# A two-layer decoder trunk on one core: opening on x by columns, and folding attention's two key blocks into one

## The chip, the cores and the metric

The kernel runs on one core of a Trainium2 chip. TensorE (PE in the profile; PEld is its weight load) multiplies, VectorE (DVE) and ScalarE (ACT) do the elementwise work, GpSimd (POOL) does a little of it, and SyncE's queue (SP) issues nearly all DMA. The metric is device microseconds of one execution. Three runs of the kernel before took 1168.31, 1168.37 and 1169.77 us, median 1168.37 us.

## What is computed

x is 256 tokens of 1024 features in float32. Two layers follow one another, each with an FFN of half weight, a mixing sub-layer and a second FFN:

```python
def rms_norm(x, g):
    y = x32 * lax.rsqrt(jnp.mean(x32 * x32, axis=-1, keepdims=True) + RMS_EPS)
    return y * g

for l in range(DEPTH):
    h = rms_norm(x, ffn1_pre_g[l])
    x = x + 0.5 * rms_norm(swiglu(h, ffn1_w1[l], ffn1_w2[l]), ffn1_post_g[l])   # (silu(h@g) * (h@u)) @ w2
    h = rms_norm(x, mix_pre_g[l])
    q, k, v, u_s, v_s, g_a, g_b = jnp.split(h @ w_in[l], IN_SPLIT_POINTS, axis=-1)
    y_attn = sliding_window_attention(q, k, v, attn_sinks[l])
    y_sgu = spatial_gating(gelu(u_s), gelu(v_s), sgu_ln_g[l], sgu_ln_b[l], sgu_w[l], sgu_b[l])
    merged = sigmoid(g_a) * (y_attn @ w_attn_branch[l]) + sigmoid(g_b) * (y_sgu @ w_sgu_branch[l])
    x = x + rms_norm(merged @ w_out[l], mix_post_g[l])
    h = rms_norm(x, ffn2_pre_g[l])
    x = x + 0.5 * rms_norm(swiglu(h, ffn2_w1[l], ffn2_w2[l]), ffn2_post_g[l])
```

The attention has 16 query heads and 2 key heads. A query at position i of a block of 128 sees the keys 0 <= i - j < 128: in its own block the keys j <= i, in the block before it the keys j > i (the first block has none before it). So each position of a key block, 0 to 127, is seen by a query in exactly one of the two blocks. A sink logit of each head joins the softmax's sum.

## The kernel before

**Precision.** Every matrix product of the trunk is made of three: each operand is split into a high part (rounded to fp32r) and a low part (the rest), and high*high + high*low + low*high is accumulated. A weight unit is 128x1024 floats (512 KB). It is loaded by SP into one of four `raw` buffers (L122), ACT casts it to its high part (L145), DVE subtracts for its low part (L154), and the units go through a ring of nine. `Stream.upto` puts these steps into the program; units are numbered in the order of the stream. The load of unit u waits until the low part of unit u-4 is made.

**Order.** The program is written out by hand: every engine runs its instructions in the order in which the code emits them. PE, ACT and DVE are in step only through semaphores.

**Opening (L1019 to L1190).** The first FFN's first eight units (four column chunks, gate and up) are multiplied token-major: x is the stationary operand, so x must lie by columns, which PE makes by transposing (16 transposes, L256). To start early, these products take x without its norm's factor r; the gain is put into four of the weight units while splitting (L149, L158) and into half of x (L1139, L1141), and `xu` holds that x as high and low parts (L1064, L1067). 17 transposes of the identity (L1091) run ahead of the data. After 96 products (8 units x 12) x's norm is known; x is scaled by it and split again into `xt`, which all later products of the FFN read. `finish` applies r, as a column per token, to the gate and the up half.

**Middle of an FFN (L678).** 18 pairs of units follow, feature-major. A pair's 32 products (L313) are 14 with 512 columns on the high parts, 16 with 256 columns on the low parts, 2 with 512 columns. After each pair ACT copies (L689), DVE adds (L690), ACT takes silu (L692) on the gate half, again copy and add on the up half, DVE multiplies (L693), then `upto` splits two more units, up to seven units ahead of the pair, and the result is split (L208, L209). With pair k (units 2k+6 and 2k+7), the splitting has gone on to unit 2k+14. After the third pair `early` loads two gains, the sinks and the gating tables for the next stage (L264, L1208, L724, L728).

**Mixing.** Products go on PE one unit at a time; beside them small tasks run at half steps of a unit (`at`, `go`). `attend` handles one of the two token blocks n and four heads per call, eight calls per layer, at the half steps of `ATTEND`. A call: scores on PE (L773, or L776 and L777), mask and maximum on DVE (L788), exponentials on ACT (L799), reciprocal and scaling on DVE (L804), transposes on PE (L811), high and low part of the transposed probabilities (L208, L209), products with v (L820, L821), and their evacuation. For n = 1 the scores have 256 keys, and the transposes, the splits and the products come once per key block: eight transposes.

## Time and profile before

| | |
|---|---|
| runs shown, median | 1168.37 us |
| profiled execution | 1168.46 us |
| its span, first to last instruction | 1166.7 us |
| mean granted TensorE clock | 0.998 |
| PE busy | 1157.3 us (99%) |
| DVE busy | 864.4 us (74%) |
| ACT busy | 704.6 us (60%) |
| POOL busy | 33.2 us (3%) |

The profiled execution's time is 1.8 us more than its span, and 0.1 us above the median of the runs. A row of the timeline gives start, duration, engine, line, operation, output<-inputs and count; the bracket at its end is the engine's idle time before it and what ended it. A row of the chain of waits gives start, duration and what the chain ran through. "PE mm" is a matmul, an "x4" behind a row merges four instructions in a row. Starts of matmuls in a row are closer together than one takes, so the cost of one is the step from start to start.

### The profile page before, as it was taken

The numbers are of one execution on the slowest core, as the hardware profiler recorded it, in microseconds if no ns is written. First come the engines' busy times: TensorE is split into PE (matmuls) and PEld (weight loads), VectorE is DVE, ScalarE is ACT, GpSimd is POOL, SyncE is SP. The second block draws the span as 40 slices with busy tenths as digits, with TensorE's granted clock in tenths as the row PEclk, the third lists the DMA queues.
The fourth block names the chain that finished last, engine by engine and source line by source line (L and its number), as shares of the span: only waits on it lengthen the run. The fifth ranks groups of instructions, "written<-read, shape, count | busy, mean of one in ns | idle before, by whom it ended". The sixth has DMA issues, their size and how long they took to land.

```text
span 1166.7 us, 16473 instructions
## 1 busy us (share of the span) xinstructions
PE 1157.3 (99%) x6005; PEld 989.5 (85%) x6005; DVE 864.4 (74%) x1491; ACT 704.6 (60%) x1215; POOL 33.2 (3%) x30
## 2 busy tenths in 40 slices
PE   9999999999999999999999999999999999999997
PEld 7888888888888888888888888888888888888886
DVE  6758758899887867666576667588999887676752
ACT  6657644679795466555455665455797954555551
POOL 0000000000021000000000000000000220000000
PEclk9999999999999999999999999999999999999999
DMA  7566674554657346557635656745555672565560
GB/s 253 185 249 219 235 250 145 194 169 144 199 164 250 127 144 217 184 200 265 218 108 187 228 199 229 232 153 179 181 167 161 201 239 66 181 208 201 197 206 36
DMA packets 61423, 220.76 MB, mean 189 GB/s; under 512 B 7072, under 2 KB 7072, under 8 KB 61344
## 3 DMA queue, kind: packets, MB, share of 16 engines
q1 hardware_dynamic: 61056, 219.46, 56.2%
q8 instruction: 47, 0.77, 0.3%
q14 instruction: 32, 0.26, 0.1%
q10 hardware_dynamic: 288, 0.27, 0.1%
HBM read 218.65 MB, written 1.05 MB: 188 GB/s over the span
## 4 chain that ended last, share of the span: by engine, by line
PE 98%; DVE 1%; ACT 1%; DMA 0%; issue 0%; DVEq 0%; POOL 0%; POOLq 0%; ACTq 0%
PE mm L291 50%; PE mm L313 42%; PE mm L256 2%; PE mm L811 1%; PE mm L744 1%; PE mm L821 0%; PE mm L820 0%; DMA raw<-in_w_in 0%; PE mm L777 0%; PE mm L776 0%; PE mm L1091 0%; PE mm L773 0%; DVE wl L154 0%; ACT m L145 0%; PE mm L278 0%
## 5 line engine op out<-in xcount | busy, mean ns | idle before, releaser
L154 DVE TENSOR_TENSOR wl<-raw,wh 128x1024 fp32r<-128x1024 f32 x370 | 447.7, 1232 | 84.7 <-ACT wh L145 82.3
L145 ACT CAST wh<-raw 128x1024 fp32r<-128x1024 f32 x370 | 381.3, 1052 | 138.2 <-DMA raw<-in_ffn_w 69.9
L291 PE MATMUL mm<-wh,m 128*128 128x512 f32 x1088 | 341.7, 391 | 0.0
L313 PE MATMUL mm<-xt,wh 128*128 128x512 f32 x1408 | 340.2, 391 | 0.0
L313 PEld LDWEIGHTS mm<-xt,wh 128*128 128x128 f32 x1408 | 257.6, 188 | 48.9
L291 PEld LDWEIGHTS mm<-wh,m 128*128 128x128 f32 x1088 | 204.3, 188 | 42.1
L291 PE MATMUL mm<-wl,m 128*128 128x512 f32 x544 | 211.8, 389 | 0.0
L313 PEld LDWEIGHTS mm<-xt,wl 128*128 128x128 f32 x1408 | 180.5, 191 | 6.9
L313 PE MATMUL mm<-xt,wl 128*128 128x256 f32 x1408 | 182.6, 283 | 0.0
L291 PE MATMUL mm<-wh,xt 128*128 128x512 f32 (+1 forms) x480 | 146.4, 380 | 0.0
L690 DVE TENSOR_TENSOR t<-mm,t 128x256 f32<-128x256 f32 x144 | 61.0, 424 | 101.8 <-ACT t L689 101.8
L291 PEld LDWEIGHTS mm<-wl,m 128*128 128x128 f32 x544 | 102.2, 188 | 20.4
L689 ACT COPY t<-mm 128x256 f32<-128x256 f32 x144 | 52.3, 363 | 88.5 <-PE mm L313 88.3
L291 PEld LDWEIGHTS mm<-wh,xt 128*128 128x128 f32 x480 | 88.4, 188 | 15.8
L291 PE MATMUL mm<-wl,xt 128*128 128x512 f32 (+1 forms) x240 | 87.5, 376 | 0.0
L692 ACT ACTIVATE t<-t 128x256 f32<-128x256 f32 x72 | 30.1, 418 | 47.8 <-DVE t L690 47.8
L291 PE MATMUL mm<-m,xt 128*128 128x512 f32 x216 | 53.5, 393 | 0.0
L291 PEld LDWEIGHTS mm<-wl,xt 128*128 128x128 f32 x240 | 45.3, 189 | 7.6
L291 PEld LDWEIGHTS mm<-m,xt 128*128 128x128 f32 x216 | 39.7, 188 | 8.7 <-ACT xt L578 1.0
L209 DVE TENSOR_TENSOR m<-t,m 128x256 fp32r<-128x256 f32 x72 | 30.2, 419 | 13.5 <-ACT m L208 13.5
L216 ACT ACTIVATE t<-mm 128x512 f32<-128x512 f32 x24 | 14.3, 598 | 40.9 <-PE mm L291 40.5
L154 DVE TENSOR_TENSOR m<-raw,m 128x1024 fp32r<-128x1024 f32 x20 | 25.8, 1329 | 13.5 <-ACT m L145 13.5
(154 smaller groups left out, 886.1 us busy)
## 6 DMA issues: line engine op xcount, KB each, us to landing
raw<-in_ffn_w SPq DMA_DIRECT2D x263, 512.0 KB, 4.3
raw<-in_w_in SPq DMA_DIRECT2D x84, 512.0 KB, 4.0
raw<-in_w_sgu_branch SPq DMA_DIRECT2D x16, 512.0 KB, 3.5
raw<-in_w_attn_branch SPq DMA_DIRECT2D x16, 512.0 KB, 3.5
raw<-in_w_out SPq DMA_DIRECT2D x16, 512.0 KB, 4.5
gain<-in_ffn_post_g SPq DMA_DIRECT2D x4, 512.0 KB, 6.7
gain<-in_ffn_pre_g SPq DMA_DIRECT2D x3, 512.0 KB, 6.4
x<-in_x SPq DMA_DIRECT2D x4, 256.0 KB, 5.0
```

Of the source, the lines that this page charges most:

```text
L145: nc.scalar.copy(h, self.raw[u])
L154: nc.vector.tensor_tensor(out=lo, in0=self.raw[u], in1=f(h), op=ALU.subtract)
L209: nc.vector.tensor_tensor(out=lo, in0=src, in1=f(h), op=ALU.subtract)
L216: nc.scalar.activation(junk, src, AF.Square, accum_out=parts[:, h:h + 1])
L256: nc.tensor.transpose(ps[:, k, :], src[:, (c0 + k) * P:(c0 + k + 1) * P], ident)
L291: nc.tensor.matmul(o, every[i][0], every[i][1], start=start and i == 0, stop=stop and i == 2)
L313: nc.tensor.matmul(out_, w[:, k * P:(k + 1) * P], x, start=k == 0 and whole, stop=k == KD - 1 and whole)
L689: nc.scalar.copy(y[:, half, :], o[half][:, S:2 * S])
L690: nc.vector.tensor_tensor(out=y[:, half, :], in0=o[half][:, 0:S], in1=y[:, half, :], op=ALU.add)
L692: nc.scalar.activation(y[:, 0, :], y[:, 0, :], AF.Silu)
L744: nc.tensor.matmul(ps[:, i, n, :], vs[:, n, (g + i) * P:(g + i + 1) * P], self.wt[:, g + i, :], start=True, stop=True)
L811: nc.tensor.transpose(ps[:, i * P:(i + 1) * P], p[:, i, c * P:(c + 1) * P], ident)
```

## The change

**The opening.** x comes from HBM by columns as well, as an array `x_cols` that the host lays out from x (a transposition of an input, no arithmetic). Four loads of 256 KB bring it; ACT and DVE scale it by the gain and split it into `xt` directly (`split0`), without the norm's factor. The opening's 96 products and all 18 pairs of the first FFN read this `xt`. The first eight units alternate between gate and up, so that one pair of x's columns serves two units. x by rows (two loads of 512 KB) is loaded later, behind unit 7, for the sum of squares and the residual. The norm's factor r is applied behind the products: for the chunks of the opening in the silu's scale, for the other 18 by one more DVE multiplication per pair on the gate half, with r spread over all partitions (`rb`). The up half is not scaled: the FFN's output is then 1/r too large per token, which the following norm takes out, with its epsilon divided by r squared (`eps01`). The 16 transposes of x are gone, the 17 transposes of the identity are 15.

**Attention, n = 1.** After mask and maximum, the two key blocks' masked scores are folded by an elementwise maximum into one block of 128 (the masked one of each two is below -1e29). Exponentials, sum and scaling go over 129 columns in place of 257, and one block is transposed: four transposes. Afterwards GpSimd separates the high and the low part again by position: `affine_select` writes a copy that keeps the keys of the block before and zeroes the others, and zeroes the complement in place. Four products with v follow, as before. The calls with n = 1 come third to sixth in a layer in place of third, fourth, seventh and eighth.

Core of the diff:

```diff
+    def open(self, n):
+            for u in range(n):
+                self.raw[u] = new(rawp, [P, 1024], "raw")
...
     def finish(self, t, r, hts, plain=False):
...
-            if r is None:
-                nc.scalar.activation(s, o[0], AF.Silu)
+            if r is None or plain:
+                nc.scalar.activation(s, o[0], AF.Silu, scale=1.0 if r is None else r)
                 nc.vector.tensor_tensor(out=hh, in0=s, in1=o[1], op=ALU.mult)
...
-        def middle(self, xt, xth, xtl, turn1, early):
+        def middle(self, xt, xth, xtl, turn1, early, scale=None):
...
                     nc.vector.tensor_tensor(out=y[:, half, :], in0=o[half][:, 0:S], in1=y[:, half, :], op=ALU.add)
+                    if half == 0 and scale is not None:
+                        nc.vector.tensor_tensor(out=y[:, 0, :], in0=y[:, 0, :], in1=scale, op=ALU.mult)
...
-            p = new(t4, [P, 4, nk + 1], "t4")
+            p = new(t4, [P, 4, P + 1], "t4")
+            both = p[:, :, 0:P] if n == 0 else new(t4, [P, 4, 2 * P], "t4")
...
+            if n == 1:
+                nc.vector.tensor_tensor(out=p[:, :, 0:P], in0=both[:, :, 0:P], in1=both[:, :, P:2 * P], op=ALU.max)
...
-            parts = []
-            for c in range(n + 1):
-                ps = bank()
-                for i in range(4):
-                    nc.tensor.transpose(ps[:, i * P:(i + 1) * P], p[:, i, c * P:(c + 1) * P], ident)
...
+            ps = bank()
+            for i in range(4):
+                nc.tensor.transpose(ps[:, i * P:(i + 1) * P], p[:, i, 0:P], ident)
+            parts = [new(t2, [P, 512], "t2", F32R) for _ in range(2)]
+            split(*parts, ps)
+            todo = [(x, n) for x in parts]
+            if n == 1:
+                for x in parts:
+                    y = new(t2, [P, 512], "t2", F32R)
+                    todo.append((y, 0))
+                    for z, sign, op in ((y, 1, ALU.is_gt), (x, -1, ALU.is_ge)):
+                        nc.gpsimd.affine_select(out=z.rearrange("p (a b) -> p a b", a=4),
+                                                in_=f(x).rearrange("p (a b) -> p a b", a=4), compare_op=op, fill=0.0,
+                                                base=0, pattern=[[0, 4], [-sign, P]], channel_multiplier=sign)
...
-            calls = [(g, n, list(range(h, h + 4))) for g in range(NKV) for n in range(NT)
+            calls = [(g, n, list(range(h, h + 4))) for g, n in ((0, 0), (0, 1), (1, 1), (1, 0))
...
+    st.open(2)
+    load_cols(0, 2)
+    for b in halves():
+        nc.sync.dma_start(st.raw[0][:, b], st.src[0][:, b])
+    nc.sync.dma_start(st.raw[1], st.src[1])
+    load_cols(2, 2)
+    st.load(RAW)
+    load_cols(4, 2)
...
+    def split0(k):
+        x, g = x_cols(k)[:, 0, :], g0[:, k:k + 1]
+        nc.scalar.activation(xt[0][:, k, :], x, AF.Copy, scale=g)
+        nc.vector.scalar_tensor_tensor(out=xt[1][:, k, :], in0=x, scalar=g, in1=f(xt[0][:, k, :]), op0=ALU.mult,
+                                       op1=ALU.subtract)
...
+    for u in range(2):
+        for i, b in enumerate(halves()):
+            if u == 0:
+                split0(i)
+            st.high(u, b)
+            st.lower(u, b)
+            for j in (0, 2, 1):
+                some(u, ((i, j),))
+        st.release(u)
+        if u == 0:
+            load_cols(6, 2)
+    for u in range(2, 8):
...
+        if u == 3:
+            for t in range(NT):
+                nc.sync.dma_start(xs[t], a["x"][rows_of(t)])
+        units(u)
...
+    st.upto(10)
+    st.low()
+    rb = spread(dg, n8, "n8")
+    subs[0].prepare()
+    turns = [first.finish(t, r01[t], subs[0].into, True) for t in range(NT)]
     st.upto(8 + AHEAD)
...
+    arrays["x_cols"] = arrays["x"].T.reshape(KD // 2, 2, P, S).transpose(0, 2, 1, 3)
```

PE in the opening, before, from its first instruction on (mm are PSUM banks, m_6 the first weight unit, n_14 and n_15 the high and low part of x):

```order
L1091 MATMUL mm_144<-ident_99 128x128 x11
L256 MATMUL mm_160<-ident_99,x_2_104 128x128 x4
L1091 MATMUL mm_144<-ident_99 128x128 x6
L291 MATMUL mm_140<-m_6_110,n_14_136 128x512 x2
L256 MATMUL mm_177<-ident_99,x_3_105 128x128 x4
L291 MATMUL mm_140<-m_6_110,n_15_137 128x512
```

And now (xt holds both parts of x; m_8 is the first unit, L272 the product that was L291):

```order
L1091 MATMUL mm_139<-ident_99 128x128 x15
L272 MATMUL mm_140<-m_8_111,xt_138 128x512
L272 MATMUL mm_142<-m_8_111,xt_138 128x512
L272 MATMUL mm_140<-m_8_111,xt_138 128x512
L272 MATMUL mm_142<-m_8_111,xt_138 128x512
```

No transpose of x stands between the products any more, and the first product has only the 15 transposes of the identity before it.

PE in the mixing, where a call with n = 1 ends and the next one's transposes follow, before (t_594 to t_598 are the parts of the transposed probabilities, vv the values, t_589 the next call's probabilities):

```order
L820 MATMUL mm_3103<-t_594_2981,vv_2121 128x512
L821 MATMUL mm_3103<-t_595_2982,vv_2121 128x512
L820 MATMUL mm_3103<-t_597_2990,vv_2121 128x512
L821 MATMUL mm_3103<-t_598_2991,vv_2121 128x512
L811 MATMUL mm_3108<-ident_99,t_589_2947 128x128 x4
L811 MATMUL mm_3117<-ident_99,t_589_2947 128x128 x4
```

And now, for a call with n = 1 and the next one's transposes (L818 was L820 and L821, L801 was L811):

```order
L818 MATMUL mm_3306<-t_652_3216,vv_2102 128x512
L818 MATMUL mm_3306<-t_653_3217,vv_2102 128x512
L818 MATMUL mm_3306<-t_654_3220,vv_2102 128x512
L818 MATMUL mm_3306<-t_655_3223,vv_2102 128x512
L801 MATMUL mm_3311<-ident_99,t_647_3184 128x128 x4
```

Four of the eight transposes are gone; the four products with v stay. t_652 to t_655 are written by GpSimd now.

DVE in the first FFN's middle, after one pair, before (t_127 is the pair's gate and up half, m_96 the low part of the result):

```order
L690 TENSOR_TENSOR t_127_627<-mm_579,t_127_627 128x256
L690 TENSOR_TENSOR t_127_627<-mm_580,t_127_627 128x256
L693 TENSOR_TENSOR t_127_627<-t_127_627 128x256
L154 TENSOR_TENSOR wl_572<-raw_514,wh_571 128x1024
L154 TENSOR_TENSOR wl_635<-raw_520,wh_634 128x1024
L209 TENSOR_TENSOR m_96_456<-t_127_627,m_95_455 128x256
```

And now (n_76 is r spread over the partitions):

```order
L675 TENSOR_TENSOR t_112_522<-mm_488,t_112_522 128x256
L677 TENSOR_TENSOR t_112_522<-t_112_522,n_76_389 128x256
L675 TENSOR_TENSOR t_112_522<-mm_489,t_112_522 128x256
L680 TENSOR_TENSOR t_112_522<-t_112_522 128x256
L137 TENSOR_TENSOR wl_481<-raw_420,wh_480 128x1024
L137 TENSOR_TENSOR wl_531<-raw_426,wh_530 128x1024
```

One multiplication (L677) stands between the first addition and the silu that ACT takes of its result.

More of the change, by code (lines that the diff above doesn't have):

```diff
@@ L53 @@
 TURN1 = 1
-WARM = (11, 6)
+WARM = 15
 ATTEND = (17, 23, 29, 35, 41, 47, 54, 60)
@@ L190, in low @@
                 self.lower(u)
-                del self.raw[u]
-                self.load(u + 1 + RAW)
+                self.release(u)
         def __getitem__(self, u):
@@ L663, in __init__ @@
             w1, w2 = a[f"ffn{i}_w1"][l], a[f"ffn{i}_w2"][l]
-            self.first = FirstFFN(l, i, early)
+            self.first = FirstFFN(l, i, early, l == 0 and i == 1)
             n = 2 * (FC - FA)
@@ L1071, in trunk, with some @@
         first.begin(t)
-        one.append(first.steps(t, *xu)[3])
-    def some(u, t, which):
-        for k, i in which:
-            one[t](u // 4, u % 4 * 2 + k, (i,))
+        one.append(first.steps(t, *xt)[3])
+    def some(u, which):
+        for t in range(NT):
+            for k, i in which:
+                one[t](u % 2, u // 2 * 2 + k, (i,))
     SOON, LATE = ((0, 0), (0, 2), (1, 0)), ((0, 1), (1, 1), (1, 2))
     def units(u):
-        for which in (SOON, LATE):
-            for t in range(NT):
-                some(u, t, which)
@@ L1088, in warm @@
-    def warm(n):
-        for _ in range(n):
-            nc.tensor.transpose(cold[:, 0:P], ident, ident)
-    cold = bank()
+        some(u, SOON)
+        some(u, LATE)
     table = new(tiny, [P, 1], "rt")
     nc.scalar.activation(table, ident[:, 0:1], AF.Copy)
-    warm(WARM[0])
-    turned, src0 = {}, {}
-    parts = [new(tiny2, [P, 2], "parts") for _ in range(NT)]
-    def turn0(t, h):
-        turned[t, h] = src0[t, h] = transpose4(xs[t], h * 4)
-    def square0(t, h):
-        square(parts[t], h, xs[t][:, halves()[h]])
@@ L1173, in normed @@
-    def normed(t, h):
-        low0(xt, t, h, xg[t][:, h * 4:h * 4 + 4, :])
-    norm(0, 0)
-    norm(0, 1)
-    normed(0, 0)
-    st.slip = True
-    st.upto(9)
-    norm(1, 0)
-    normed(0, 1)
-    norm(1, 1)
-    normed(1, 0)
-    normed(1, 1)
-    units(6)
-    units(7)
+    for _ in range(WARM):
+        nc.tensor.transpose(cold[:, 0:P], ident, ident)
+    for u in range(2):
[9 more added lines that the diff above has]
+            load_cols(6, 2)
@@ L1189, in trunk @@
+    dg = diagonal(r01)
+    eps01 = [new(const, [P, 1], f"eps{t}") for t in range(NT)]
+    for e, v in zip(eps01, sums):
+        nc.vector.tensor_scalar(out=e, in0=v, scalar1=RMS_EPS, scalar2=None, op0=ALU.mult)
+    st.slip = True
+    st.upto(10)
[3 more added lines that the diff above has]
+    turns = [first.finish(t, r01[t], subs[0].into, True) for t in range(NT)]
     st.upto(8 + AHEAD)
-    subs[0].prepare()
-    turns = [first.finish(t, r01[t], subs[0].into) for t in range(NT)]
@@ L1210, in early @@
                 nxt.tables()
-        behind = sub.middle(both, *xt, turn1, early)
-        turn1 = project(sub.rows, sub.lhs, sub.k_post, gains[0], None if last else gains[1], nxt, xt, behind)
+        behind = sub.middle(both, *xt, turn1, early, *([flat(rb)] if i == 0 else []))
+        turn1 = project(sub.rows, sub.lhs, sub.k_post, gains[0], None if last else gains[1], nxt, xt, behind,
+                        *([eps01] if i == 0 else []))
 def kernel(**inputs):
```

185 lines of the change are left out of this document (49 added, 136 removed).

## The prediction

> **What bounds the kernel now.** I read the page first: busy shares and the chain of waits by engine.
>
> ```profile
> PE 1157.3 (99%) x6005; PEld 989.5 (85%) x6005; DVE 864.4 (74%) x1491; ACT 704.6 (60%) x1215; POOL 33.2 (3%) x30
> PE 98%; DVE 1%; ACT 1%; DMA 0%; issue 0%; DVEq 0%; POOL 0%; POOLq 0%; ACTq 0%
> ```
>
> The chain runs through PE for 98% of the span. A modelled PE busy of 99% proves little, so I looked for what PE waited for (engine, line, releaser: us, times, longest):
>
> ```profile
> PE mm L1091 <- POOL ident masks.py:199: 1.4, 1, 1.4
> PE mm L291 <- ACT n L1064: 0.4, 1, 0.4
> PE mm L256 <- DVE t L509: 0.2, 1, 0.2
> PE mm L291 <- ACT m L145: 0.2, 1, 0.2
> ```
>
> In the whole span PE waits visibly 2.2 us, nearly all of it at the start. So a matmul taken out anywhere behind the opening is worth its step from start to start, as long as nothing new makes PE wait; and work added to DVE, ACT or POOL is free until it makes PE wait. That leaves two places to look at: the opening, and the rows where the margin is thin. The opening in the chain of waits, in order of time:
>
> ```profile
> 1.42 2.61 PE mm L1091 x11
> 4.03 0.85 PE mm L256 x4
> 4.89 1.17 PE mm L1091 x6
> 6.06 0.46 PE mm L291 x2
> ...
> 10.97 1.15 ACT t L1139 x4
> ...
> 22.82 0.67 PE mm L278 x2
> 23.50 8.19 PE mm L291 x36
> 31.69 16.68 PE mm L313 x96
> ```
>
> The first product stands at 6.06, the first pair of the middle at 31.69: 25.6 us. The 96 products need 96 x 8.19/36 = 21.8 us of that, the spreading of r (L278) 0.7, the 12 transposes of x that lie between 12 x 0.11 = 1.3 (step from the row of 307.86 below). The remaining 1.8 us PE stands still, for ACT above all, which prepares x (10.97).
>
> **The opening, term by term.** When can the first product start now? Issues, landings (the last number of a row is us from issue to landing), ACT's first work, and what DMA moved in the first 60 us, in 40 slices of 1.5:
>
> ```profile
> 0.80 0.40 ACTq L1021 DMA_DIRECT2D g<-in_gain  x1
> g<-in_gain ACTq DMA_DIRECT2D x1, 4.0 KB, 3.0
> 1.72 0.42 SPq L1023 DMA_DIRECT2D x<-in_x  x1
> x<-in_x SPq DMA_DIRECT2D x1, 256.0 KB, 4.4
> 4.40 0.72 ACT L149 ACTIVATE m<-raw,g 128x512 fp32r<-128x512 f32 x1 [1.67 <-DMA raw<-in_ffn_w]
> 5.03 0.56 ACT L1064 CAST n<-mm 128x512 fp32r<-128x512 f32 x1
> 2.66 0.43 SPq L122 DMA_DIRECT2D raw<-in_ffn_w  x1
> raw<-in_ffn_w SPq DMA_DIRECT2D x1, 512.0 KB, 5.4
> GB/s 0 181 289 329 359 401 415 300 295 221 8 232 358 377 202 240 76 295 276 57 0 0 169 412 388 407 208 360 145 19 5 52 363 262 66 311 295 49 98 309
> ```
>
> The first two loads keep their sizes and places in SP's queue (256 KB of x, 256 KB of unit 0). The gain is there at 3.8; scaling 256 columns takes some 0.43 us (estimate, a little over half of L149's 0.72), so it ends before unit 0's first half lands at 4.4. Its cast (0.56 to 0.63) ends at 5.0. PE's 15 transposes end at 1.42 + 15 x 2.61/11 = 5.0. First product: 5.0, which is 1.1 earlier.
>
> PE's step is long at first: 0.21 us per transpose at 4.03, 0.20 on average at 4.89, but a product at 6.06 takes 0.23 as later ones do. It became short around 5.8. Products between 5.0 and 5.8 then run at half speed: 0.4 us lost.
>
> The Trainium skill, "TensorE: Matmul & The Clock Gate", section "Part 4: PE-mode transpose", says that transposes do not count as activity for the clock gate, so that a stretch of transposes alone would not open it. The trace disagrees: only transposes ran before 6.06, and the product there has its full speed. By the rule the first products would stay slow; that is a rival below.
>
> Next: unit 0's second half is the third load now; the third load before was issued at 1.72 and landed 4.4 later, at 6.1. Its cast ends at 6.7, the first six products at 5.0 + 0.4 + 6 x 0.23 = 6.8: no wait. Unit 1 (512 KB) is fourth. The 512 KB issued at 2.66 as the fifth load landed at 8.1; half a microsecond earlier and 256 KB less ahead of it I take 7.4 (halves cast by 8.0 and 8.6), against products of unit 0 that end at 8.1. Were it 8.1 as before, PE would wait 0.5. I take 0.1. From there on a unit's 12 products (2.7 us) are longer than its cast, its subtraction and two columns' scaling on either engine (ACT 1.05 + 0.9, DVE 1.2 + 0.9). At the end PE must spread r, which needs x by rows, four sums of squares and a chain of small DVE operations, some 4 us behind the last row (estimate from two squares of 0.8 and some twenty operations of 0.1 to 0.2 us in the profile). PE wants it at 27.3, so x has to be in by 23.3, and with it eight units and x by columns, 6.3 MB. At the mean from 3 to 12 us (349 GB/s) it is in at 20; at the mean of the first 20 slices (246), in which SP often waited for a free buffer, at 25.6, which would be 2.3 late. The queue holds x by rows behind unit 7 and nothing else waits in front, so I take no wait.
>
> Sum: 5.0 + 0.4 + 0.1 + 21.8 + 0.7 = 28.0, against 31.69: **3.7 us**. Bounds: 4.2 without the slow stretch and the wait; 3.7 - 0.4 - 2.3 = 1.0 with a late unit 1 and late rows of x.
>
> **Attention.** The stretch in the mixing where a second-block call's transposes stand, with DVE's splitting and the two lines of GpSimd selects (us busy, mean ns):
>
> ```profile
> 296.47 0.23 PE mm L820
> ...
> 297.39 0.87 PE mm L811 x8
> 298.26 2.74 PE mm L291 x12
> ...
> 306.94 0.23 PE mm L820
> 307.86 0.44 PE mm L811 x4
> 287.55 1.28 DVE L209 TENSOR_TENSOR t<-mm,t 128x512 fp32r<-128x512 f32 x2
> 301.26 1.28 DVE L209 TENSOR_TENSOR t<-mm,t 128x512 fp32r<-128x512 f32 x2
> L725 POOL TENSOR_SCALAR_AFFINE_SELECT wt<-wt 128x1024 f32<-128x1024 f32 x2 | 2.2, 1119 | 326.5 <-DMA wt<-in_sgu_w 326.5
> L1044 POOL TENSOR_SCALAR_AFFINE_SELECT mask<-mask 128x128 f32<-128x128 f32 x1 | 0.3, 292 | 0.1
> 340.72 1.48 DVE L154 TENSOR_TENSOR wl<-raw,wh 128x1024 fp32r<-128x1024 f32 x1 [2.08 <-ACT wh L145]
> ```
>
> Four transposes cost 0.44 and eight 0.87, with PE unbroken on either side. Eight calls (four per layer) lose four each: 8 x 0.435 = **3.5 us**. The four products with v stay. Removed exponential columns, one cast and one subtraction per call relieve ACT and DVE, off the path: nothing.
>
> What could take it back? A select of 512 columns was never run here; between 292 ns for 128 and 1119 for 1024, on a line, it is 0.65 us. Behind the low part (ready at 302.5) three selects must still follow, 1.95 us, and the products that read them stood at 306.94: 4.4 us. The call before has 7.6 (288.8 to 296.47). Hidden; the cover ends at 1.5 us per select.
>
> DVE's fold writes the tile that the previous call's transposes still read (two buffers now hold two tiles per call), so DVE waits there for PE, with the weight subtractions queued behind it. But DVE runs behind PE here: the splitting of transposes that PE ended at 298.26 starts at 301.26. I cost the wait at nothing.
>
> POOL may also hold DVE up: the subtraction at 340.72 took 1.48 us, against 1.23 as the mean of its line, when POOL was at work. Sixteen selects a layer by 0.65 are at most 10 us of DVE over some 45 us; the subtractions run up to seven units of 2.7 us ahead of their products, so that is not yet a wait.
>
> The Trainium skill, "SBUF — State Buffer", section "Who interferes with whom", says that a DVE operation with two SBUF inputs and a GpSimd operation that reads SBUF lock each other out. The 1.48 agrees.
>
> **The late norm** adds one DVE multiplication in front of the silu in each of 18 pairs. Here the margin is thin:
>
> ```profile
> 43.12 0.41 DVE L690 TENSOR_TENSOR t<-mm,t 128x256 f32<-128x256 f32 x1
> 44.28 0.43 DVE L690 TENSOR_TENSOR t<-mm,t 128x256 f32<-128x256 f32 x1 [0.74 <-ACT t L689]
> 44.74 0.43 DVE L693 TENSOR_TENSOR t<-t 128x256 f32<-128x256 f32 x1
> 47.69 0.42 DVE L690 TENSOR_TENSOR t<-mm,t 128x256 f32<-128x256 f32 x1
> 73.47 1.05 ACT L145 CAST wh<-raw 128x1024 fp32r<-128x1024 f32 x1 [8.80 <-DMA raw<-in_ffn_w]
> 76.23 2.00 ACT L145 CAST wh<-raw 128x1024 fp32r<-128x1024 f32 x2
> 76.47 3.82 PE L313 MATMUL mm<-xt,wh 128*128 128x512 f32 x16
> ```
>
> A round on DVE is 47.69 - 43.12 = 4.57 us, and PE's pair 5.57. One more dependent operation costs 0.46 (44.28 to 44.74): 5.03, still shorter than the pair. But ACT and DVE start late, and the loads of gains and tables hold up unit 24 until 73.4. By the count of the rounds the casts at 76.23 are those of units 25 and 26. Pair 9 begins two products into the row of 76.47, at 76.9, and reads unit 25 seven products later, at 78.5; its cast ends at 77.3. The margin is **1.2 us**.
>
> With the opening 3.7 shorter, PE reads unit 25 at 74.8. The loads of gains and tables stand behind the third round. That now starts earlier too: behind the opening's end at 28.0 ACT copies r, loads a table and takes two silus (0.4 + 1.3 + 1.3), unit 10 is cast and subtracted (1.0 + 1.2), only then unit 14 is loaded and cast (4 + 1.0), and the first round's copy follows (estimate from durations of the same operations): DVE starts near 38.5, against 43.1. Less 3 x 0.46 for three rounds, 3.2 us earlier; one more 0.46 for unit 25, which is then ready at 74.6. That is 0.2 in hand, uncertain by a microsecond. I take a wait of 0.3, bounds 0 and 3.0 (unit 25 not earlier at all: 77.3 + 0.5 - 74.8).
>
> **Sum.** The profiled execution's 1168.46 (span and 1.8 around it) - 3.7 - 3.5 + 0.3 = 1161.6; the median of the runs is 0.1 lower: **1161.5 us**, 0.6% less. Its own range is 1160.4 to 1163.
>
> **Rivals.**
>
> *The opening's gain is stopped at pair 9.* For it: the margin, and tables that must come. Against: they are issued earlier as well. PE then gains 1.2 - 0.5 = 0.7 us of the 3.7: 1168.4 - 3.5 - 0.7 = 1164.2. Chance 0.14.
>
> *A cold or hungry opening.* Were the clock not opened by transposes, the products would have to open it, in about the time from 1.42 to 5.8, at half speed: 2.2 us lost in place of 0.4. Late rows of x cost up to 2.3. The one gives 1163.3, the other 1163.8. The first is what the rule of the Trainium skill's "TensorE: Matmul & The Clock Gate" (above) would do here. Against it: the product at 6.06; against the late rows: 349 GB/s. Chance 0.10.
>
> *The change gives nothing.* DVE, held by the fold's wait and by POOL, falls so far behind that PE waits some 0.9 us in each of the eight calls: 1168.5. For it: the 1.48 us, and the fold's wait. Against: the lead of seven units. Chance 0.09.
>
> *Slower: the selects.* If a select in this form (four blocks of 128, result in fp32r) took 3 us, three of them would be 9 us, against distances of 7.6 and 4.4 between splitting and products, 6.0 in the mean: 3 us in each of eight calls, 24 in all, 1185. From about 2.4 us per select it outweighs the gain. Against: L725 has the same pattern of blocks at 1.1 ns per column. Chance 0.05.
>
> The forecast has 0.62. 1164.2, 1163.3 and 1163.8 are faster too: 0.86 for faster by over 0.2% (2.3 us), about what a measurement of this kernel can tell from no change; within it 0.09, slower 0.05. The range 1160.0 to 1166.0 holds the first three cases.
>
> **What would show it.** First product near 5.0 and first pair near 28.0 in the chain; no wait of PE between; a select near 0.65 us; one row of four transposes per call; PE's waits on ACT at pair 9 below a microsecond; DVE's fold without idle time before it. I am wrong if PE waits for POOL in the mixing, or for casts around 73 to 76.

## The result, and the profile after

The changed kernel takes 1163.04 us, median of five runs (1161.98 to 1163.72), against 1168.34 us before: a ratio of 0.995, 95% interval 0.9939 to 0.9961. It is 5.3 us faster. The forecast was 1161.5, 6.9 us faster, with its own range from 1160.4 to 1163: the median stands at its upper end, 0.04 us outside. Five more runs in a later comparison gave a median of 1162.84; the median of all ten is 1162.9, just inside.

The profiled execution took 1161.98 us with a span of 1160.2, so it is the fastest of its five and 6.5 us below the profiled one of before. Its busy shares and its chain of waits by engine:

```profile
PE 1150.5 (99%) x5955; PEld 983.5 (85%) x5955; DVE 870.5 (75%) x1498; ACT 692.8 (60%) x1201; POOL 61.9 (5%) x62
PE 89%; DVE 6%; ACT 3%; issue 1%; DMA 1%; DVEq 0%; ACTq 0%
```

PE's share of the chain fell from 98% to 89%: DVE and ACT now have stretches in which the end hangs on them. What PE waits for, in the whole span (us, times, longest):

```profile
PE mm L1091 <- POOL ident masks.py:199: 1.4, 1, 1.4
PE mm L801 <- ACT n L953: 0.6, 2, 0.3
PE mm L272 <- ACT m L133: 0.3, 1, 0.3
PE mm L764 <- DVE t L190: 0.3, 1, 0.3
```

Two waits are new, and both stand in the mixing: the transposes (L801) wait for ACT's copy of another product (L953), and the scores of the second block (L764) for DVE's low part of an earlier call (L190). The opening in the chain of waits:

```profile
0.80 2.95 DMA g<-in_gain
3.77 0.51 ACT xt L1061
4.28 0.59 ACT m L133
4.92 22.14 PE mm L272 x96
27.05 0.43 PE mm L259 x2
27.48 4.53 PE mm L294 x25
```

The first product starts at 4.92, its 96 products run without a gap of note, and the first pair starts at 27.48 against 31.69: 4.2 us earlier.

Where the rest of the gain lies is seen best by matching products. Both kernels have the same 5504 products with weights in the same order, so the n-th start in one trace can be set against the n-th in the other. This table gives the lead over the kernel before, in us, at the first pair, before and behind the stretch of attention's calls in each layer, and at the last product; the last column is what the two stretches of calls gained together. The rows below the first belong to the experiments that follow.

```
                            first  layer 1, calls   layer 2, calls   last     both
                            pair   before  behind   before  behind   product  stretches
changed kernel              4.20    4.56    5.34     5.38    6.45     6.55     1.85
changed kernel, again       3.25    3.61    4.63     4.77    5.62     5.68     1.87
attention alone            -0.18    0.15    0.88     0.89    2.01     2.01     1.84
opening alone               3.69    4.07    4.14     4.30    4.29     4.36     0.07
old order of calls          2.95    3.28    3.39     3.46    3.66     3.67     0.30
no selects                  3.78    4.08    5.83     5.61    7.40     7.48     3.54
selects twice               3.55    3.68    0.11    -0.17   -3.19    -3.15    -6.60
no transposes ahead         1.54    1.92    2.99     2.91    3.89     3.99     2.05
two calls later             3.43    3.27    4.94     5.12    6.74     6.84     3.30
two calls later, again      3.15    3.21    4.57     4.27    5.71     5.81     2.80
two calls later, halves     3.27    3.25    4.81     4.87    6.31     6.41     3.00
two selects, DVE and ACT    3.19    3.53    2.76     2.61    2.32     2.38    -1.04
two selects, GpSimd         3.52    3.69    5.24     5.32    7.00     7.07     3.23
```

The eight calls with n = 1 were to give 3.5 us. They gave 1.85. The opening gave 4.2 in this execution, but ten profiled executions with the changed opening (all of the table but attention alone, no transposes ahead, and the one with halves, whose loads differ) lie between 2.95 and 4.20, with a median of 3.5. The profiled execution has the best opening of the ten. With 3.5 for the opening and 1.85 for attention, and 0.3 gained in small pieces elsewhere (the median over the same profiles), the sum is 5.65, close to the 5.3 of the medians.

### The profile page after: what moved, and what is told of

It is laid out like the page before. It is cut to its first block, busy times and chain, and to the rows that moved or that the text cites. A ratio compares the mean times of both kernels' runs of the same rounds, so it can differ in the third digit from the quotient of the medians.

```text
span 1160.2 us, 16444 instructions
## 1 busy us (share of the span) xinstructions
PE 1150.5 (99%) x5955; PEld 983.5 (85%) x5955; DVE 870.5 (75%) x1498; ACT 692.8 (60%) x1201; POOL 61.9 (5%) x62
## 4 chain that ended last, share of the span: by engine, by line
PE 89%; DVE 6%; ACT 3%; issue 1%; DMA 1%; DVEq 0%; ACTq 0%
PE mm L272 47%; PE mm L294 38%; DVE wl L137 2%; PE mm L237 1%; ACT wh L133 1%; DVE t L777 1%; ACT t L791 1%; DMA raw<-in_w_in 0%; PE mm L818 0%; PE mm L731 0%; PE mm L801 0%; DVE t L888 0%; DVE t L783 0%; DMA g<-in_gain 0%; DVE m L742 0%
## 5 line engine op out<-in xcount | busy, mean ns | idle before, releaser
L137 DVE TENSOR_TENSOR wl<-raw,wh 128x1024 fp32r<-128x1024 f32 x372 | 451.6, 1236 | 83.2 <-ACT wh L133 81.5
L272 PE MATMUL mm<-wh,m 128*128 128x512 f32 x1088 | 341.6, 391 | 0.0
L272 PEld LDWEIGHTS mm<-wh,m 128*128 128x128 f32 x1088 | 204.3, 188 | 41.7
L272 PE MATMUL mm<-wl,m 128*128 128x512 f32 x544 | 211.7, 389 | 0.0
L272 PE MATMUL mm<-wh,xt 128*128 128x512 f32 (+1 forms) x512 | 155.1, 381 | 0.0
L272 PEld LDWEIGHTS mm<-wl,m 128*128 128x128 f32 x544 | 102.2, 188 | 20.7
L272 PEld LDWEIGHTS mm<-wh,xt 128*128 128x128 f32 x512 | 94.4, 188 | 16.9
L272 PE MATMUL mm<-wl,xt 128*128 128x512 f32 (+1 forms) x256 | 92.4, 376 | 0.0
L272 PE MATMUL mm<-m,xt 128*128 128x512 f32 x264 | 64.8, 393 | 0.3 <-ACT m L133 0.3
L272 PEld LDWEIGHTS mm<-m,xt 128*128 128x128 f32 x264 | 48.6, 188 | 11.1 <-ACT xt L561 1.0
L272 PEld LDWEIGHTS mm<-wl,xt 128*128 128x128 f32 x256 | 48.3, 189 | 8.2
L811 POOL TENSOR_SCALAR_AFFINE_SELECT t<-t 128x512 fp32r<-128x512 f32 x32 | 28.8, 911 | 478.7 <-ACT t L189 462.4
L137 DVE TENSOR_TENSOR m<-raw,m 128x1024 fp32r<-128x1024 f32 (+1 forms) x24 | 28.6, 1222 | 14.8 <-ACT m L133 14.5
L190 DVE TENSOR_TENSOR m<-t,m 128x256 fp32r<-128x256 f32 x72 | 30.1, 417 | 12.6 <-ACT m L189 12.6
```

Of the source, the lines that this page charges most:

```text
L137: nc.vector.tensor_tensor(out=lo[:, b], in0=self.raw[u][:, b], in1=f(h[:, b]), op=ALU.subtract)
L190: nc.vector.tensor_tensor(out=lo, in0=src, in1=f(h), op=ALU.subtract)
L272: nc.tensor.matmul(o, every[i][0], every[i][1], start=start and i == 0, stop=stop and i == 2)
L811: nc.gpsimd.affine_select(out=z.rearrange("p (a b) -> p a b", a=4), in_=f(x).rearrange("p (a b) -> p a b", a=4), compare_op=op, fill=0.0, ...
```

## Experiments

### One part at a time

Attention alone: the kernel before with the changed kernel's `attend`, whole, and its order of the calls (shown). Opening alone: the changed kernel with the `attend` and the order of the kernel before.

```diff
-            calls = [(g, n, list(range(h, h + 4))) for g in range(NKV) for n in range(NT)
+            calls = [(g, n, list(range(h, h + 4))) for g, n in ((0, 0), (0, 1), (1, 1), (1, 0))
```

> The opening of the kernel before, the attention of the changed one (fold, selects, four transposes, new order of the calls). Theory A (the attention loses part of its own gain to two waits of PE per layer for PSUM banks, whatever the opening does): those waits show here too, before the scores of the fifth call and the transposes of the sixth, and the kernel is 1.9 us faster than before, 3.5 from the transposes less 1.6 from the waits: 1166.4. Rival B (the waits come only because the shorter opening brings PE to the mixing 4.6 us earlier): no such wait, 3.5 us faster, 1164.8.

> The opening of the changed kernel, the attention of the kernel before (eight transposes, old order of the calls, no selects). Theory A: the first pair of the middle starts at 27.5, the lead of 4.2 us over the kernel before grows to 4.6 at the end of the first FFN and is held through the mixing, with no wait of PE for banks: 4.6 us faster, 1163.7. Rival B: the lead itself causes waits in the mixing, about 1.6 us over two layers: 3.0 us faster, 1165.3. By the prediction's own term: 3.7 us less 0.3, 1164.9.

Attention alone took 1166.45 us (ratio 0.9981, 0.9972 to 0.999), 2.0 us faster than the 1168.47 of before beside it. PE's waits in it:

```profile
PE mm L814 <- ACT n L966: 0.6, 2, 0.3
PE mm L777 <- DVE t L209: 0.2, 1, 0.2
```

These are the two waits of the changed kernel under other line numbers (L814 the transposes, L966 the copy, L777 the scores, L209 the low part). So they do not come from the shorter opening; theory A holds, and attention costs itself half of its gain.

The opening alone took 1164.21 us (0.9964, 0.9951 to 0.9976), 4.3 us faster. Its lead is 3.69 at the first pair, 4.1 just ahead of the first calls and 4.36 at the end: nothing of it is lost in the mixing, and PE waits there for nothing. The expected 4.6 was taken from the one execution with the best opening. 2.0 and 4.3 make 6.3, a little more than the 5.3 to 5.8 of both together; the spread of the openings is as large as this difference.

### Which of attention's edits takes the gain back

```diff
-            calls = [(g, n, list(range(h, h + 4))) for g, n in ((0, 0), (0, 1), (1, 1), (1, 0))
+            calls = [(g, n, list(range(h, h + 4))) for g in range(NKV) for n in range(NT)
```

> The changed kernel with the calls of attention in the old order: two calls of the first block, two of the second, twice. Theory A1 (four calls of the second block in a row load DVE with four long maxima and folds in a row; it falls behind, and PE waits for the banks that it reads): with the old order DVE can catch up between, the two waits per layer vanish, 1.6 us faster than the changed kernel: 1161.4. Rival A2 (the selects hold DVE up, or the fold is too much for any order): waits of 0.3 to 0.5 us remain, at other calls, and the time stays near 1163.

```diff
                 for x in parts:
-                    y = new(t2, [P, 512], "t2", F32R)
-                    todo.append((y, 0))
-                    for z, sign, op in ((y, 1, ALU.is_gt), (x, -1, ALU.is_ge)):
-                        nc.gpsimd.affine_select(out=z.rearrange("p (a b) -> p a b", a=4),
-                                                in_=f(x).rearrange("p (a b) -> p a b", a=4), compare_op=op, fill=0.0,
-                                                base=0, pattern=[[0, 4], [-sign, P]], channel_multiplier=sign)
+                    todo.append((x, 0))
```

> The changed kernel without the selects: the high and the low part go into the products with v of both key blocks as they are, so that the separation of the two blocks is left out of the computation; the count of products, transposes and folds is the same. Theory A2 (GpSimd's selects hold DVE up while they run: DVE's weight subtraction takes 1.65 us beside them in place of 1.23): the waits of PE before the scores of the fifth call and the transposes of the sixth vanish or shrink below 0.1 us, 1.6 us faster than the changed kernel, 1161.4. Rival A1 (order and fold): the waits stay as they are, 1163.

With the old order of the calls the kernel took 1164.08 us (0.9964, 0.9952 to 0.9977), no better than the changed one. Its opening was the slowest of the ten (2.95), but its stretches of calls gained only 0.3 us in place of 1.85. PE's waits, then GpSimd's and PE's rows at the last call of layer 1, from the timeline:

```profile
PE mm L818 <- POOL t L811: 1.8, 2, 0.9
PE mm L761 <- DVE t L190: 0.4, 2, 0.2
```

```profile
335.42 3.54 POOL L971 TENSOR_TENSOR n<-n,n 128x512 f32<-128x512 f32 x2 [1.24 <-ACT n L968]
338.91 4.66 POOL L811 TENSOR_SCALAR_AFFINE_SELECT t<-t 128x512 fp32r<-128x512 f32 x4
342.33 0.39 PE L818 MATMUL mm<-t,vv 128*128 128x512 f32 x1
343.63 0.96 PE L818 MATMUL mm<-t,vv 128*128 128x512 f32 x3 [0.91 <-POOL t L811]
```

The selects of the last call queue behind the gate's multiplications (L971) on GpSimd and end too late for the products with v (L818). The new order of the calls keeps the selects out of that place; it is worth some 1.5 us. The waits for banks shrink from 0.9 us in the view to 0.4, so the order has a part in them, but they do not vanish, as theory A1 had it, and the time is not 1161.4. What is left of A1 falls with the next run, which keeps the new order and the fold.

The next kernel leaves out the separation of the two key blocks, and so computes something else with as many products, transposes and folds. Without selects the kernel took 1161.38 us (0.9938, 0.9926 to 0.9951), 1.5 us faster than the median of the changed kernel's ten runs. Its stretches of calls gained 3.54 us, the prediction's eight times 0.435, and PE waits in them for nothing. So the selects are the cause, and the fold, the new order and everything else in the change cost nothing. Nor do they act by holding the buffers that DVE and ACT write: neither engine waits for GpSimd in the view of the changed kernel's waits. How they act is seen in the busy time of the engines in 40 us of the mixing (span, then PE, PEld, DVE, ACT and POOL with their instruction counts; of the kernel before, of the changed one and of the one without selects, each at the same stretch of its work):

```profile
284.50:324.50 40.00, 40.00 (x205) 33.85 (x204) 35.99 (x83) 32.24 (x77) 0.00 (x0) 1.00 0.51 161
```

```profile
280.00:320.00 40.00, 39.41 (x196) 32.78 (x195) 38.29 (x80) 29.95 (x71) 14.57 (x16) 1.00 0.50 162
```

```profile
280.00:320.00 40.00, 40.00 (x201) 33.65 (x200) 35.78 (x80) 30.92 (x75) 0.00 (x0) 1.00 0.54 164
```

DVE, busy for 74% of the whole span, was at 90% in this stretch already before; the selects bring it to 96%. The groups of DVE's instructions in these 40 us (busy us, mean ns of one), first of the changed kernel, then without selects (there L830 is what L835 is here):

```profile
L137 DVE TENSOR_TENSOR wl<-raw,wh 128x1024 fp32r<-128x1024 f32 x12 | 15.5, 1290 | 0.8 <-ACT wh L133 0.7
L777 DVE CUSTOM_DVE_ANT_0 t<-mm,mask,sinks 128x256 f32<-128x256 f32 x12 | 5.1, 481 | 0.1
L835 DVE TENSOR_TENSOR m<-t,m 128x256 fp32r<-128x256 f32 x4 | 3.0, 740 | 0.0
L190 DVE TENSOR_TENSOR t<-mm,t 128x512 fp32r<-128x512 f32 x4 | 2.7, 683 | 0.3 <-ACT t L786 0.3
L796 DVE TENSOR_TENSOR t<-t,rd 128x512 f32<-128x512 f32 x3 | 2.5, 841 | 0.1
```

```profile
L137 DVE TENSOR_TENSOR wl<-raw,wh 128x1024 fp32r<-128x1024 f32 x12 | 14.6, 1221 | 0.8 <-ACT wh L133 0.7
L777 DVE CUSTOM_DVE_ANT_0 t<-mm,mask,sinks 128x256 f32<-128x256 f32 x12 | 5.1, 483 | 0.1
L190 DVE TENSOR_TENSOR t<-mm,t 128x512 fp32r<-128x512 f32 x4 | 2.7, 686 | 1.9 <-ACT t L189 1.9
L796 DVE TENSOR_TENSOR t<-t,rd 128x512 f32<-128x512 f32 x3 | 2.1, 693 | 0.1
L830 DVE TENSOR_TENSOR m<-t,m 128x256 fp32r<-128x256 f32 x4 | 1.7, 419 | 0.0
```

Operations with two inputs from SBUF are stretched (740 against 419 ns, 841 against 693, 1290 against 1221); those with an input from PSUM (L190, L777) are not. The smallest operation is stretched most for its length, although it has a single input from SBUF: the negated maximum at the third call, first in the changed kernel, then without selects.

```profile
283.21 0.60 DVE L785 TENSOR_SCALAR nm<-m 128x4 f32<-128x4 f32 x1
```

```profile
283.51 0.16 DVE L785 TENSOR_SCALAR nm<-m 128x4 f32<-128x4 f32 x1
```

The sharing is mutual: over 32 selects one takes (ns min/median/max, in the changed kernel)

```profile
L811 POOL TENSOR_SCALAR_AFFINE_SELECT t<-t x32: 637/816/1503, 283.0 to 892.5; 128x512 fp32r<-128x512 f32 x32
```

0.64 us beside a DVE operation that reads PSUM (the select at 315.62, beside L190) and 1.50 where it starts beside a weight subtraction (those at 286.89, 298.61 and 308.96, beside L137). This is the rule of the Trainium skill, "SBUF — State Buffer", section "Who interferes with whom": a DVE instruction with two SBUF inputs contends with a GpSimd instruction that reads SBUF; one with at most one SBUF input does not, outside the modes in which DVE takes both port pairs. The two groups of rows agree with both halves; by L785 not every operation with one SBUF input is exempt, and the trace does not show in which mode it ran.

From a late DVE to a waiting PE it goes over PSUM. In the chain of waits of the changed kernel, around the two waits of layer 1:

```profile
284.40 0.61 DVE t L190
...
285.15 0.36 PE mm L764
...
307.47 0.10 DVE t L783
...
308.33 1.66 ACT t L791 x8
...
311.73 2.00 ACT wh L133 x2
313.73 0.48 ACT n L953
...
314.26 0.63 PE mm L801 x4
```

Scores have no use for the low part of another call's probabilities, nor transposes for the copy of a gate's product: what they share is one of the eight PSUM banks, which are handed out in turn. DVE's low part (L190) is late, not least for the 0.60 us of L785 two operations ahead of it, so its bank is, and the scores wait 0.4 us from start to start. DVE's maximum and fold (L783) are late, so ACT's exponentials (L791) are, and behind them in ACT's queue three casts, two other copies and the copy (L953), and the transposes wait 0.5 us. In the kernel without selects the same products wait for nothing: the same fold starts 1.1 us earlier, ACT's copy too (312.52 in place of 313.63), and the transposes at 313.78 in place of 314.26.

```profile
306.36 0.69 DVE L783 TENSOR_TENSOR t<-t 128x512 f32<-128x512 f32 x1
```

### How much cover the selects have

```diff
-                    for z, sign, op in ((y, 1, ALU.is_gt), (x, -1, ALU.is_ge)):
+                    for z, sign, op in ((y, 1, ALU.is_gt), (y, 1, ALU.is_gt), (x, -1, ALU.is_ge), (x, -1, ALU.is_ge)):
```

> The changed kernel with each select made twice in a row (the second repeats the first and changes nothing): 64 selects in place of 32. If selects act on the time only through DVE, which they hold up (the products with v stay covered), the loss of 1.6 us doubles at most: 1163 to 1165. By the prediction's cover, six selects behind the low part at the measured 0.64 to 1.5 us are about 5.5 us against a distance of some 4: PE also waits for POOL ahead of the products with v, about 2 us in the fourth and fifth call of each layer, 8 us in all: about 1171.

It took 1171.14 us (1.0022, 1.0012 to 1.0031), slower than before, and as the prediction's cover had it. PE's wait, and GpSimd's and PE's rows at the fourth call of layer 1:

```profile
PE mm L818 <- POOL t L811: 7.0, 4, 2.5
```

```profile
299.99 6.62 POOL L811 TENSOR_SCALAR_AFFINE_SELECT t<-t 128x512 fp32r<-128x512 f32 x6 [3.04 <-DVE t L190]
306.66 0.96 PE L818 MATMUL mm<-t,vv 128*128 128x512 f32 x3 [2.49 <-POOL t L811]
```

Six selects behind the low part take 6.62 us, 2.2 for what was one select, and PE waits for them. With selects made once the three take some 3.3 us in the fourth call of layer 1 and in its fifth and end 0.9 and 0.6 us ahead of their products: the cover is there, but it is thin.

### Half of the selects

The products with v can do with one select per part: P times v0 - v1 splits into the whole part times v0 and the own block's keys times the difference v1 - v0. The difference takes the place of v1; it costs four small operations per layer. In the first of two runs they stand on DVE and ACT, in the second on GpSimd, both at unit 10 of the mixing.

```diff
+            nc.vector.tensor_tensor(out=d, in0=f(vv[:, 1]), in1=f(vv[:, 0]), op=ALU.subtract)
+            nc.scalar.copy(vv[:, 1, :, 0, :], d[:, :, 0, :])
+            nc.vector.tensor_tensor(out=d[:, :, 0, :], in0=d[:, :, 0, :], in1=f(vv[:, 1, :, 0, :]), op=ALU.subtract)
+            nc.vector.tensor_tensor(out=vv[:, 1, :, 1, :], in0=d[:, :, 0, :], in1=d[:, :, 1, :], op=ALU.add)
...
+                todo = [(x, 0) for x in parts]
                 for x in parts:
                     y = new(t2, [P, 512], "t2", F32R)
-                    todo.append((y, 0))
-                    for z, sign, op in ((y, 1, ALU.is_gt), (x, -1, ALU.is_ge)):
-                        nc.gpsimd.affine_select(out=z.rearrange("p (a b) -> p a b", a=4),
-                                                in_=f(x).rearrange("p (a b) -> p a b", a=4), compare_op=op, fill=0.0,
-                                                base=0, pattern=[[0, 4], [-sign, P]], channel_multiplier=sign)
+                    todo.append((y, 1))
+                    nc.gpsimd.affine_select(out=y.rearrange("p (a b) -> p a b", a=4),
+                                            in_=f(x).rearrange("p (a b) -> p a b", a=4), compare_op=ALU.is_ge,
+                                            fill=0.0, base=0, pattern=[[0, 4], [1, P]], channel_multiplier=-1)
```

> The changed kernel with half of the selects: the products with the first block's v take the whole parts, and those with the difference of the two blocks' v (four small operations per layer more) take a copy that keeps only the own block's keys. 16 selects, none in place, so that only one follows the low part. Theory A2 (selects hold DVE up): the bank waits shrink to less than half, and the kernel comes to 1161.4 to 1162.2. Rival (any select at that place is enough to make DVE late, or the waits come from the order of the calls): 1163.

> The changed kernel with half of the selects, as the run with two selects before, but the four operations for the difference of v stand on GpSimd, at half step 20, where it is idle, in place of DVE and ACT. Theory A2 (the selects' hold on DVE causes the bank waits): the waits shrink below half, 1161.4 to 1162.2. Rival (two selects are as bad as four): 1163.

The first took 1166.01 us (0.9976, 0.9968 to 0.9985), 3 us more than the changed kernel: it missed both expectations. DVE and PE in its timeline:

```profile
250.90 0.42 DVE L749 TENSOR_TENSOR t<-vv 128x256 f32<-128x256 f32 x1
252.46 0.29 DVE L751 TENSOR_TENSOR t<-t,vv 128x128 f32<-128x128 f32 x1 [1.14 <-ACT vv L750]
263.08 1.16 PE L294 MATMUL mm<-xt,wh 128*128 128x512 f32 x4 [0.75 <-DVE m L786]
```

and among PE's waits in the whole span

```profile
PE mm L294 <- DVE m L786: 2.0, 3, 0.8
PE mm L773 <- DVE t L190: 1.2, 2, 0.6
```

The second of the four operations waits 1.14 us for ACT's copy, whose queue is busy with casts. DVE loses 2.1 us there (0.42 + 1.14 + 0.29 + 0.29), and within some ten microseconds PE's products wait for its maxima (L786), 2.0 us over both layers. The scores' wait for the low part's bank (L773) is there as well, and longer than with all selects: 1.2 us in all against 0.3. Whether it too comes from the four operations, the run does not show; with them on GpSimd (below) it is gone. So this run told nothing about the selects, but it told how little DVE has in hand: work of 2 us per layer put on it there came back on PE.

With the four operations on GpSimd it took 1161.5 us (0.9939, 0.9925 to 0.9952). The stretches of calls gained 3.23 us of 3.5, and PE waits in the mixing for nothing that the view shows. Half of the selects is enough to keep DVE in time.

### Moving the two calls that wait

```diff
-ATTEND = (17, 23, 29, 35, 41, 47, 54, 60)
+ATTEND = (17, 23, 29, 35, 42, 48, 54, 60)
```

> The changed kernel with the fifth and the sixth call of attention half a unit (1.4 us) later (half steps 42 and 48 in place of 41 and 47). Theory (PE waits there only for PSUM banks whose readers are 0.2 to 0.5 us late): both waits are covered and do not come back elsewhere, 1.6 us faster than the changed kernel: 1161.4. Rival (DVE is behind over the whole stretch; the waits move to the next bank or to POOL ahead of the products with v): no gain, 1163 or more.

> The changed kernel once more, as the measure for the other three of this group on the same chip. 1163.0 by its first five runs; its mixing loses 1.6 us in PE's two bank waits per layer, and its opening's end lies between 27.5 and 28.8, by when unit 1 lands.

> The fifth and the sixth call half a unit later, beside the changed kernel on the same chip. Theory: faster than the changed kernel by the 1.6 us of the bank waits, 1161.4. Rival (the 1.0 us between the two medians so far is the spread of the openings): no more than 0.5 us.

Two comparisons gave 1161.98 (0.9943, 0.9931 to 0.9956) and 1162.32 us (0.9946, 0.9934 to 0.9959), the changed kernel again in the second of them 1162.84 (0.9948, 0.9935 to 0.996). The ten runs of the two have a median of 1162.24, against 1162.88 for ten of the changed kernel: 0.6 us. On the same chip it is 0.5, about what the rival allowed and not the 1.6 expected. The two profiles gained 3.30 and 2.80 us in the stretches, and the wait of the transposes is gone in both, while that of the scores stays in the second (L764, 0.2 us once). Moving a call covers the wait, but does not make DVE earlier. Both profiles also have a wait of 0.3 us for DVE just ahead of the mixing (L237 for L492), which the two of the changed kernel do not have. By the stretches in the profiles it is worth 0.9 to 1.5 us, by the medians on the same chip 0.5. Part of this difference lies outside the span from first to last instruction: the time is 2.0 to 2.1 us more than the span in the five runs beside the changed kernel, and 1.7 to 1.8 in those of the changed kernel. By the median spans, 1160.2 and 1161.1, the gain is 0.9 us. Why the time outside grew, no run shows; and the spread of the openings, 1.2 us in these runs, is as large as the gain.

### The opening

```diff
-WARM = 15
+WARM = 0
```

> The changed kernel without the 15 transposes of the identity ahead of the first product. Theory T (transposes open the clock: steps of 0.21 us at first, 0.11 later): the first products now run at half speed until some 3.5 us of work are done, about 1.8 us are lost at the opening: first pair near 29.5 in place of 27.5 to 28.0, 1164.8. Rival R (transposes count for nothing, only products do): the products behind 4.9 are as fast or slow as with the transposes, no change: 1163.

Its profiled execution took 1164.54 us, its median is 1163.46 (0.9955, 0.9939 to 0.997). PE in its timeline, and in that of a kernel with the 15 transposes (the one with halves, below):

```profile
4.91 7.35 PE L272 MATMUL mm<-m,xt 128*128 128x512 f32 x19 [4.91 <-ACT m L133]
```

```profile
5.00 7.35 PE L272 MATMUL mm<-m,xt 128*128 128x512 f32 x27
```

In the same 7.35 us, 19 products without transposes ahead and 27 with them. Without, the first thirteen have steps of 0.43 us and the step falls to 0.23 only between 10.6 and 11.0; with transposes it falls between 4.3 and 7.3, in two executions still among the transposes. The first pair starts at 30.14, 1.9 us later than the median of the others; theory T had 1.8. The times do not show it in full, and the 1164.8 expected is missed by the median: the other three runs lie at 1163.2 to 1163.5, 0.3 to 0.6 above the changed kernel's median. Whether in those the short step came sooner, the runs do not tell.

```diff
-    nc.sync.dma_start(st.raw[1], st.src[1])
+    for b in halves():
+        nc.sync.dma_start(st.raw[1][:, b], st.src[1][:, b])
```

> As the kernel with the two calls later, and unit 1 loaded in two halves of 256 KB as unit 0 is. Theory (PE waits for unit 1's first half, 0.4 to 0.8 us in most of the profiled openings): its cast no longer waits for the second half's data, the wait at the thirteenth product is gone, 0.4 us faster: 1161.0 to 1161.5. Rival (the extra issue of 0.4 us on SP puts off every later load, or the halves land when the whole did): same or slower by up to 0.4.

It took 1161.09 us (0.9937, 0.9924 to 0.9949), the fastest of all, 1.2 us less than the same kernel without this edit on the same chip; 0.4 was expected. ACT's casts of unit 1 with one load (the first of the two runs with the calls moved), in the timeline, and PE's remaining products in the chain of waits:

```profile
7.80 1.14 ACT L133 CAST m<-raw 128x512 fp32r<-128x512 f32 x2 [1.41 <-DMA raw<-in_ffn_w]
```

```profile
8.47 19.36 PE mm L272 x84
```

And ACT's casts with two loads (the first of the three is unit 0's second half):

```profile
6.01 1.94 ACT L133 CAST m<-raw 128x512 fp32r<-128x512 f32 x3 [0.66 <-DMA raw<-in_ffn_w]
```

With one load ACT waits until 7.8 and PE's thirteenth product until 8.47; with two, unit 1's first half follows straight behind unit 0's second, and PE's step there is 0.24. But the short step came only at 7.0 in this execution, the longest of its five, so the products were late themselves; with one load and a short step as late, in the second run with the calls moved, PE does not wait at unit 1 either. The wait with one load is 0.6 us at most in the profiles, so it cannot be the whole of the 1.2. The halves bring the casts forward, and the median is lower; that the one is the cause of the other, and of all of it, is not shown. By the medians this kernel is 7.6 us faster than before and 1.8 faster than the changed one; the intervals of its ratio and of the changed kernel's overlap a little, so the second number is the less certain one. Together with half of the selects it was not run.

## Why the prediction was right, and where it was not

**The opening: 3.7, measured 2.95 to 4.20, median 3.5.** The first product was put at 5.0 and stands at 4.87 to 5.27. The chain goes there through the gain's 4 KB (2.9 to 3.3 us from issue to landing), ACT's scaling and the cast of unit 0, as worked out, though the gain and not the unit comes last. The 0.4 for the slow step was 0.1 to 1.1. The wait for unit 1, costed at 0.1 because it was to land at 7.4, is 0 to 0.6: it landed between 6.8 and 8.3. The late rows of x, up to 2.3 in the bounds, cost nothing: behind the thirteenth product the remaining 84 run in 19.36 us, 0.23 each. So the value was good and the spread was not foreseen. The 4.2 of the profiled execution is luck: of all openings its step was short earliest, and unit 1 came in time.

**The pair 9 wait: 0.3, measured 0.** From the timeline of the changed kernel, ACT's casts of units 25 and 26, and PE's products:

```profile
71.27 2.00 ACT L133 CAST wh<-raw 128x1024 fp32r<-128x1024 f32 x2
72.30 3.82 PE L294 MATMUL mm<-xt,wh 128*128 128x512 f32 x16
```

Unit 25 is ready at 72.3; pair 9 begins two products into PE's row, at 72.8, and reads it seven later, at 74.4. The margin is 2.05 us, more than the 1.2 of before. Cast and use both came 4 to 5 us earlier; the sum had put the cast only 2.7 earlier. The first rival, which had the opening's gain stopped here, is out, and the 18 multiplications of the late norm cost nothing.

**Attention: 3.5, measured 1.85.** The value of the four transposes was right: 3.54 with the selects away. The step that failed is the one on GpSimd: "the subtractions run up to seven units of 2.7 us ahead of their products, so that is not yet a wait". It looked for the damage only at the weights' low parts. Their lead did hold. But the same DVE also reads PSUM banks that PE wants back within a few microseconds, and feeds ACT, which reads others; those have no lead of seven units. Nor did it count the operations with one input from SBUF, of which L785 went from 0.16 to 0.60 us. And it took DVE's room from the whole span (74%), where in this stretch 36.0 of 40 us were taken already. The rival "the change gives nothing" had this mechanism, with DVE held by POOL; its price, 0.9 us per call, was too high by four: 1.65 over eight calls is 0.2 each. The time came near the forecast because the rest nearly held: 1.65 less from attention and 0.2 less from the opening, against 0.3 for the wait at pair 9 that did not come and the 0.3 of small pieces, which nobody forecast and no run explains.

**The select: 0.65, measured 0.64 alone and 0.9 on the mean.** Taken from rows of 128 and 1024 columns it was right for a select that DVE does not disturb. The cover, said to end at 1.5 us per select, was about right: at 2.2 the products with v wait, and the 3.3 us of three selects with 0.6 to 0.9 in hand put the end at 1.3 to 1.4. The point from which selects outweigh the gain was put at 2.4 us; the doubled ones at 2.2 were already 2.4 us slower than before, since what DVE loses comes on top of what PE waits.

**The fold's wait on PE: nothing**, as costed: DVE sat idle 0.3 us ahead of three folds in the 40 us, with and without selects.

**The cold opening** as a rival had 1163.3, near the measured time, but for another reason: only transposes ran before the first product, and its step was short by 7.3 at the latest, against 11.0 without them. The rule in the Trainium skill, "TensorE: Matmul & The Clock Gate", "Part 4: PE-mode transpose", that transposes do not count for the clock gate, does not hold for this kernel's fp32 transposes; whether they ran in the transpose mode that it speaks of, the trace does not show.

## What to carry to other kernels

A busy share over the span hides the stage in which an engine is full: before work is added beside a stage, or on an engine whose operations stretch those of a full one, read the busy time of that stage alone. A consumer that runs seven units ahead for its main job may be just in time for a small one; the readers of PSUM banks, which come round every few microseconds, have the least lead and show lateness first. A transfer that PE waits for early can be halved, so that work on its first half does not wait for the second; here that came with 1.2 us, more than the wait it was to remove.

## What the runs showed of the hardware

DVE and GpSimd hold each other up, and by much: a 128x256 subtraction with two SBUF inputs went from 419 to 740 ns on the mean of four, a 128x512 select from 0.64 to 1.50 us at most, while operations reading PSUM kept their 683 and 481 ns. A negation of four columns, with one input from SBUF, took 0.60 us beside a select in place of 0.16.

Transposes shorten PE's step as products do, from 0.21 to 0.11 us for one transpose, but when this comes varies: 4.3 to 7.3 us into the span over the profiles with the same 15 transposes from 1.4 on. At 0.43 in place of 0.23 us for a product, that alone moves the products of the opening by up to 1.1 us, of which some is covered where they would have waited for unit 1.
